# Attention values with the values standing still, two heads in the two halves of PE's columns

## The chip, the core and the metric

The kernel runs on one core of a Trainium2 chip. The metric is device time in microseconds from launch to end. Five engines work side by side and meet at semaphores: PE (matrix products; PEld is its loading of the standing operand), DVE (vector), ACT (scalar functions), POOL (here only an issuer of transfers) and SP (transfers). Each works through its own list of instructions in order.

## What is computed

One block of a decoder for 512 tokens of width 1024, in float32: a retention branch and an attention branch, both mixed by gates, and then a feed-forward layer. What matters here is the attention: 8 heads of width 64, blocks of 256 keys, of which 3 would be chosen beside a query's own block. With 512 tokens there are two blocks, so every earlier block is taken and the attention is plain causal attention:

```
mq = rmsnorm(mq, q_norm_w); mk = rmsnorm(mk, k_norm_w)        # per head, 64 wide
s_own = einsum('bhqd,bhjd->bhqj', qb, k_own) * scale           # masked where key > query
p = softmax(concatenate([s_sel, s_own], axis=-1), axis=-1)
out = einsum('bhqkj,bhqkjd->bhqd', p_sel, vs) + einsum('bhqj,bhjd->bhqd', p_own, v_own)
b = moba_attention(mq, mk, mv) @ w_moba_out
mix = sigmoid(ga) * a + sigmoid(gb) * b                        # a: the retention branch
```

## The kernel before

Nearly all of PE's work are products of activations with weights. Each operand is split into a high and a low part of type float32r, and a product is three matmuls (`mm3`). Most large products are done by a scheme of seven products in place of eight (`wino_unit`); its weights arrive as `raw` by DMA, ACT makes the high part (`wh`), DVE the low part (`wl`) and sums of weights (`wt`).

The order of everything is written out by hand. The main products go in half steps of twelve matmuls. After each half step `advance` runs what is due (`later`, then a new piece of weights), and `run_bg` takes one entry of the list `bg`, the background work. So each engine's list holds, in turn, a half step of main products, then one background entry.

The attention is such background work: 32 items (head, query tile of 128), two heads in turn, tiles 0 to 3 of a pair of heads, then the next pair. Entry `n` of the list is `att_step(n)`. With `ATT = (2, 4)` it does three things for three items:

- `att_values` for item n-4: products of `pt` with the values `mv`, 64 columns each, one per block of keys up to the diagonal; DVE writes the result, times `rl`, into `mo`
- `att_transpose` for item n-2: PE transposes the probabilities `p` block by block, ACT copies them to `pt`, DVE makes `rl = 1/l`
- `att_scores` for item n: PE makes the scores (those of two heads together for tiles 0 and 1), DVE their maximum `mx` and `nb` from it, ACT `p = exp(...)`, with the row sum `l` written when it ends

The first entry runs in the value unit `mv`, the next ones in the unit `rk` (rotary products, DVE's `rot`) and in `rv`. `mo` holds tokens by heads. Four entries `mo_steps` much later, in the last `rv` unit, transpose it (`mo_transpose`), and `split` makes the high and low part of `moT`, the input of the branch `b`. The buffers: `act` gives tiles of 512 columns out of 9, `big` tiles of 1024 columns out of 45, and PSUM has 8 banks, shared by the main products (`pm`) and the background (`ps`).

Lines of the profile: every PE and DVE instruction is recorded by a helper at L191, so tiles tell them apart. ACT's exponential is L874, the copy to `pt` L884.

Of the kernel before, what the change touches and what calls it, by code (L numbers as in the profile page):

```python
# [13 lines left out]
ALU = mybir.AluOpType  # L14
AX = mybir.AxisListType

P = 128
S = 512
D = 1024
KT = D // P  # L20
NT = S // P
# [4 lines left out]
MDH = 64  # L26
# [15 lines left out]
RLAG = (1, 2, 3)  # L42
SLAG = (1, 1, 1)
ROT = 1
MOT = 0
LATE = 1
RNORM = 4
QKS = 4
# [2 lines left out]
ATT = (2, 4)  # L51
# [87 lines left out]
def hybrid_block(ctx: ExitStack, tc: tile.TileContext, wall, xin, cin, out):  # L139
# [12 lines left out]
    def act(name, dt=F32):  # L152
        return sp.tile([P, 512], dt, name=name, tag="a")

    def big(name, dt=F32):
        return bp.tile([P, 1024], dt, name=name, tag="b")

    def halves(name, dt=F32):
        t = big(name, dt)
        return t[:, :512], t[:, 512:]  # L160

    def small(name, n, bufs=2):
        return tp.tile([P, n], F32, name=name, tag=name, bufs=bufs)
# [3 lines left out]
    def nm(s):  # L167
        uid[0] += 1
        return f"{s}_{uid[0]}"
# [4 lines left out]
    def side_ps():  # L174
        return pp.tile([P, 512], F32, name=nm("ps"), tag="bank")

    A = nc.scalar
# [22 lines left out]
    V, T = Paced(nc.vector, dve_cost), Paced(nc.tensor, pe_cost)  # L200
# [31 lines left out]
    def later(n, f):  # L232
        later_q.append([n, f])
# [122 lines left out]
    def split(name, src, scale=None, lag=0):  # L356

        lows = []

        def high():  # L360
            h, l = halves(name, F32R)
            lows.append(l)
            if scale is None:
                A.copy(h, src)
            else:
                A.activation(h, src, AF.Copy, scale=scale)
            return h

        def low(h):
            l = lows[0]  # L370
            if scale is None:
                V.tensor_tensor(l, src, h.bitcast(F32), ALU.subtract)
            else:
                V.scalar_tensor_tensor(l, src, scale, h.bitcast(F32), ALU.mult, ALU.subtract)
            return l

        p = Piece(high, low, lag, SLAG[2])
        waiting.append(p)
        return p
# [35 lines left out]
    ident = cst[:, K_ID:K_ID + P]  # L415
# [3 lines left out]
    def two(x):  # L419
        return x.rearrange("p (u c) -> p u c", u=2)  # L420
# [78 lines left out]
    for k in range(KT):  # L499
        if k % 2 == 0:  # L500
            hf[k // 2] = big(f"hf{k}")
        f = two(hf[k // 2])[:, k % 2]
        n1 = xv[:, V_N1 + k:V_N1 + k + 1]
        V.tensor_scalar(f, xt[k], n1, None, ALU.mult)
        c = slice(k % 2 * 512, k % 2 * 512 + 512)
# [58 lines left out]
    bg = []  # L564
# [252 lines left out]

    mv = {}

    mo_steps = [lambda f=f: mo_transpose(f) for f in range(4)]  # L820

    def mv_out(pair, u, x):
        for i in (0, 1):
            t = 2 * pair + i
            if i == 0 and t not in mv:
                mv[t], mv[t + 1] = halves(f"mv{t}")
            A.activation(mv[t][:, u * 256:(u + 1) * 256], x[:, i * 256:(i + 1) * 256], AF.Copy,
                         scale=st["r1"][:, t:t + 1])
        if (pair, u) == (1, 0):
            for t in (0, 2):  # L830
                mo[t], mo[t + 1] = halves(f"mo{t}")
            for n in range(len(items) + ATT[1]):
                bg.append(lambda n=n: att_step(n))
            if MOT:
                bg.extend(mo_steps)

    for _ in range(EXTRA):
        for f in load_w():
# [1 line left out]
    wino_unit(hW, Quarters(mv_out))  # L840


    mo, srg_ev = {}, {}
    items = [(2 * g + r, i) for g in range(MH // 2) for i in range(NT) for r in (0, 1)]
    att, both = {}, {}

    def score_products(h, i):

        hp, r = h // 2, h % 2
        W, d = (i + 1) * P, slice(i * P, (i + 1) * P)  # L850
        ps = side_ps()
        if i < 2:
            kh, kl = (two(x)[:, :, :W] for x in mkT[hp][:, :])
            o = ps[:, :2 * W].rearrange("p (u c) -> p u c", u=2)
            mm3(o, mqT[hp][:, d], (kh, kl), True, False)
            T.matmul(o[:, :, d], lhsT=identb, rhs=negb.unsqueeze(1).to_broadcast([P, 2, P]), start=False, stop=True)
            for x in (0, 1):
                both[2 * hp + x, i] = ps[:, x * W:(x + 1) * W]
        else:
            mm3(ps[:, :W], mqT[hp][:, d], mkT[hp][:, r * 512:r * 512 + W], True, False)  # L860
            T.matmul(ps[:, d], lhsT=identb, rhs=negb, start=False, stop=True)
            both[h, i] = ps[:, :W]

    def att_scores(h, i):
        if (h, i) not in both:
            score_products(h, i)
        W, ps = (i + 1) * P, both.pop((h, i))
        mx, nb = small("mx", 1, 4), small("nb", 1, 4)
        V.tensor_reduce(mx, ps[:, :W], AX.X, ALU.max)
        q = st["qs"][:, i * MH + h:i * MH + h + 1]  # L870
        V.tensor_scalar(nb, mx, -1.0, q, ALU.mult, ALU.mult)
        p = act(nm("p"))
        l = small("l", 1, 6)
        A.activation(p[:, :W], ps[:, :W], AF.Exp, bias=nb, scale=q, accum_out=l)  # L874
        att[h, i] = (p, l)

    def att_transpose(h, i):
        p, l = att[h, i]
        W = (i + 1) * P
        ps = side_ps()  # L880
        for j in range(i + 1):
            T.transpose(ps[:, j * P:(j + 1) * P], p[:, j * P:(j + 1) * P], ident)
        pt = act(nm("pt"))
        A.copy(pt[:, :W], ps[:, :W])  # L884
        rl = small("rl", 1, 6)
        V.reciprocal(rl, l)
        att[h, i] = (pt, rl)

    def att_values(h, i):
        pt, rl = att.pop((h, i))  # L890
        ps = side_ps()
        for j in range(i + 1):
            T.matmul(ps[:, :MDH], lhsT=pt[:, j * P:(j + 1) * P], rhs=mv[j][:, h * MDH:(h + 1) * MDH],
                     start=j == 0, stop=j == i)
        V.tensor_scalar(mo[i][:, h * MDH:(h + 1) * MDH], ps[:, :MDH], rl, None, ALU.mult)

    def att_step(n):
        if 0 <= n - ATT[1] < len(items):
            att_values(*items[n - ATT[1]])
        if 0 <= n - ATT[0] < len(items):  # L900
            att_transpose(*items[n - ATT[0]])
        if n < len(items):
            att_scores(*items[n])

    moT = {}

    def mo_transpose(f):
        ps = side_ps()
        for t in range(NT):
            T.transpose(ps[:, t * P:(t + 1) * P], mo[t][:, f * P:(f + 1) * P], ident)  # L910
        moT[f] = split(f"moT{f}", ps, None, SLAG[0])


    srg = {}
# [16 lines left out]
    def gates(n):  # L931

        ready_gates.append(n)
        for m in (0, 1):
            if ready_gates.count(m) == 2:
                ready_gates[:] = [x for x in ready_gates if x != m]
                bg.extend([None] * RGATE[m] + [lambda h=2 * m + i, p=p: ret_gate(h, p) for i in (0, 1) for p in (0, 1)])
# [52 lines left out]
    def rv_out(h0):  # L990
        def f(pair, i, x):
            rv[h0 + i, pair] = split(f"rv{h0 + i}_{pair}", x, None, 0 if (pair, i) == (1, 0) else SLAG[1])
            if (pair, i) == (1, 0):
                a, b = ([lambda h=h, j=j: ret_scores(h, j) for j in range(NT)] for h in (h0, h0 + 1))
                v, w = ([lambda h=h, p=p: ret_values(h, p) for p in range(2)] for h in (h0, h0 + 1))
                if h0 and not MOT:
                    bg.extend(mo_steps)
                bg.extend(a + b[:2] + [None, None] + v + b[2:] + [None] * 4 + w + [None])
                gates(h0 // 2)
                ret_done("rv")  # L1000
        return f
# [17 lines left out]
    def ret_scores(h, j):  # L1019

        n0 = min(j * P, 256)
        w = S - n0
        ps = side_ps()
        mm3(ps[:, :w], rkT[h][:, j * P:(j + 1) * P], rqT[h][:, n0:], True, True)
        key, off = sc_off[j]
        if off == 0:
            sc[h, key] = halves(nm("sc"), F32R)
        H, L = sc[h, key]
        d0 = j * P - n0
        s = sk[:, h * NT + j:h * NT + j + 1]  # L1030
        tmp = tp.tile([P, P], F32, name=nm("dia"), tag="dg", bufs=4)
        rest = S - (j + 1) * P
        o, d = slice(off + P, off + P + rest), slice(off, off + P)

        def first():
            V.scalar_tensor_tensor(tmp, ps[:, d0:d0 + P], s, tri, ALU.mult, ALU.mult)
            if rest:
                A.activation(H[:, o], ps[:, d0 + P:w], AF.Copy, scale=s)

        def second():  # L1040
            A.copy(H[:, d], tmp)
            if rest:
                V.scalar_tensor_tensor(L[:, o], ps[:, d0 + P:w], s, H[:, o].bitcast(F32), ALU.mult, ALU.subtract)

        later(RLAG[0], first)
        later(RLAG[1], second)
        later(RLAG[2], lambda: V.tensor_tensor(L[:, d], tmp, H[:, d].bitcast(F32), ALU.subtract))
# [343 lines left out]
```

## Time and profile before

| | |
|---|---|
| median of 3 runs | 817.28 us (816.57 to 817.59) |
| profiled execution | 817.44 us, span 815.7 us |
| PE busy | 803.1 us, 98% of the span, 5568 matmuls |
| DVE, ACT, POOL busy | 581.3, 406.3, 59.9 us |
| granted TensorE clock | 1.00 |
| attention's items, first score to last | about 88.6 to 184.8 us |
| last value products; `mo` transposed | 192.1 us; 268.8 to 274.4 us |

The span is from the first to the last instruction; the execution's own time is 1.7 us longer. A row of a group names the tile written and the tiles read (`ps<-mv,pt`), the shape, how many there are, the busy time, the mean of one in ns, and the idle time of the engine before them with what ended it. The chain is followed back from the last instruction to what released it. A single row of the timeline begins with its start and its duration in us. Matmuls are pipelined: one begins long before the one ahead has ended, so their cost in a sequence is the distance of the starts.

### The profile page before, as it was taken

To read this page: it belongs to the slowest core of one execution; us is meant where nothing else is said; L and a number is where in the kernel's file an instruction comes from. 1 tells how busy PE (TensorE), PEld (TensorE's weight loads), DVE (VectorE), ACT (ScalarE), POOL (GpSimd) and SP (SyncE) were. 2 spreads that over 40 slices of the span, in tenths; PEclk is the share of its full clock that TensorE was granted. 3 is DMA by queue.
4 is the path that set the end of the run, shared out by engine and by line. 5 is a ranking of instruction groups with operands and counts; after the bars stand their busy time and mean duration, and the time that the engine had idled before them with its cause. 6 is when DMAs were issued, how large, how long until landed. Compare 5 with 4: busy or idle time off the path is not lost.

```text
span 815.7 us, 13699 instructions
## 1 busy us (share of the span) xinstructions
PE 803.1 (98%) x5568; PEld 747.4 (92%) x5568; DVE 581.3 (71%) x889; ACT 406.3 (50%) x639; POOL 59.9 (7%) x82
## 2 busy tenths in 40 slices
PE   7998999999999999999999999999999999999998
PEld 5888999999999999998988899988999988999986
DVE  7879866786798678887666978743677665688731
ACT  8557744565447456664434466534455422455400
POOL 0004000000000000000011110000000022000000
PEclk9999999999999999999999999999999999999999
DMA  9733343162436545543747696625565676865111
GB/s 327 229 98 74 110 108 78 32 151 88 146 79 155 137 123 156 129 133 104 228 155 203 140 293 167 189 69 164 149 178 156 164 172 149 214 181 174 59 53 51
DMA packets 35839, 117.56 MB, mean 144 GB/s; under 512 B 4032, under 2 KB 4544, under 8 KB 35776
## 3 DMA queue, kind: packets, MB, share of 16 engines
q1 hardware_dynamic: 27360, 89.95, 33.4%
q0 software_dynamic: 8416, 26.74, 18.6%
q8 instruction: 43, 0.70, 0.3%
q14 instruction: 20, 0.16, 0.1%
HBM read 110.91 MB, written 4.19 MB: 141 GB/s over the span
## 4 chain that ended last, share of the span: by engine, by line
PE 95%; DVE 2%; ACT 1%; DMA 0%; issue 0%; DVEq 0%; SPq 0%; ACTq 0%
PE pm L191 86%; PE ps L191 9%; DVE wl_B L191 1%; DMA raw<-wall 0%; DVE wl_T L191 0%; ACT sqh L725 0%; ACT qk L724 0%; DVE qk L191 0%; DVE mk1l L191 0%; DVE mk0l L191 0%; DVE wt_T L191 0%; DVE ssr_y L191 0%; ACT wh_T L297 0%; DVE qb L191 0%; DVE ssr_t L191 0%
## 5 line engine op out<-in xcount | busy, mean ns | idle before, releaser
L191 PE MATMUL pm<-h2S,wh_T 128*128 128x256 f32 x528 | 96.5, 283 | 0.0
L191 PEld LDWEIGHTS pm<-h2S,wh_T 128*128 128x128 f32 x528 | 82.3, 192 | 0.0
L191 DVE TENSOR_TENSOR wl_B<-raw_B,wh_B 128x1024 fp32r<-128x1024 f32 x60 | 72.6, 1220 | 12.4 <-ACT wh_B L297 8.0
L191 DVE TENSOR_TENSOR wl_T<-wt_T,wh_T 128x1024 fp32r<-128x1024 f32 x40 | 48.9, 1223 | 43.5 <-ACT wh_T L297 41.4
L271 POOL DMA_DIRECT2D raw_T<-wall x40 | 35.0, 874 | 567.6 <-DMA raw_T<-wall 246.1
L191 PE MATMUL pm<-h2S,wl_T 128*128 128x256 f32 x264 | 74.7, 283 | 0.0
L191 PE MATMUL pm<-gh,wh 128*128 128x512 f32 x176 | 68.5, 389 | 0.0
L191 PE MATMUL pm<-gl,wh 128*128 128x512 f32 x176 | 68.5, 389 | 0.0
L191 PE MATMUL pm<-gh,wl 128*128 128x512 f32 x176 | 68.5, 389 | 0.0
L297 ACT CAST wh_B<-raw_B 128x1024 fp32r<-128x1024 f32 x60 | 62.0, 1047 | 10.8 <-PE pm L191 10.8
L191 DVE TENSOR_TENSOR wl<-raw,wh 128x1024 fp32r<-128x1024 f32 x54 | 65.5, 1219 | 1.6 <-ACT wh L297 1.3
L191 PE MATMUL pm<-h2A,wh_B 128*128 128x256 f32 x352 | 64.3, 283 | 0.0
L297 ACT CAST wh<-raw 128x1024 fp32r<-128x1024 f32 x54 | 55.4, 1044 | 11.0 <-PE pm L191 10.9
L191 DVE TENSOR_TENSOR wl_T<-raw_T,wh_T 128x1024 fp32r<-128x1024 f32 x40 | 48.8, 1221 | 16.1 <-ACT wh_T L297 10.6
L297 ACT CAST wh_T<-wt_T 128x1024 fp32r<-128x1024 f32 x40 | 41.9, 1047 | 30.9 <-DVE wt_T L191 29.4
L191 PEld LDWEIGHTS pm<-h2A,wh_B 128*128 128x128 f32 x352 | 55.1, 192 | 0.2
L297 ACT CAST wh_T<-raw_T 128x1024 fp32r<-128x1024 f32 x40 | 41.8, 1044 | 19.9 <-PE pm L191 13.2
L191 PEld LDWEIGHTS pm<-h2S,wl_T 128*128 128x128 f32 x264 | 50.7, 192 | 0.0
L191 PE MATMUL pm<-h2A,wl_B 128*128 128x256 f32 x176 | 49.8, 283 | 0.0
L191 PE MATMUL pm<-wh_T,hS 128*128 128x256 f32 x240 | 47.8, 287 | 1.2 <-ACT qa L684 1.2
L191 PE MATMUL pm<-hA,wh 128*128 128x256 f32 x256 | 47.2, 285 | 0.0
L191 PEld LDWEIGHTS pm<-wh_T,hS 128*128 128x128 f32 x240 | 39.0, 192 | 1.4 <-ACT qa L684 1.4
(276 smaller groups left out, 2153.0 us busy)
## 6 DMA issues: line engine op xcount, KB each, us to landing
raw_B<-wall SPq DMA_DIRECT2D x60, 512.0 KB, 5.1
raw<-wall SPq DMA_DIRECT2D x54, 512.0 KB, 4.1
raw_T<-wall SPq DMA_DIRECT2D x40, 512.0 KB, 3.6
raw_T<-wall POOLq DMA_DIRECT2D x40, 512.0 KB, 5.7
raw<-wall SPq DMA_DIRECT2D x8, 256.0 KB, 5.7
xr<-xin POOLq DMA_DIRECT2D x8, 256.0 KB, 5.9
x2d<-xr SPq DMA_DIRECT2D x8, 256.0 KB, 2.8
acc<-x2d POOLq DMA_DIRECT2D x8, 256.0 KB, 5.4
```

The source lines that it names most:

```text
L191: return f(out, *args, **kw)
L271: nc.gpsimd.dma_start(t[:, s], wall[c, :, s], accum_op=ALU.add)
L297: A.copy(h, src)
```

## The change

The values stand still in PE and the transposed probabilities move. For one head the standing operand is 64 columns of `mv` (one block of keys), and the moving one is `pt` for all queries from that block's own tile on: 512, 384, 256 and 128 columns. Two heads write the upper and lower 64 partitions of the same bank, which uses the two halves of PE's columns. The result of a pair of heads is `moT` as it stands, so the tile `mo` and its transposes go. For that, `pt` of a head is kept for all its query tiles (`a`, `b` in `pT[h]`), and ACT copies into it by blocks of keys. The division by the row sum moves from the result to `p`, ahead of its transposition, at the next half step (`later(1, norm)`). `att_values` runs once per pair of heads instead of once per item.

```diff
 def att_scores(h, i):
...
     A.activation(p[:, :W], ps[:, :W], AF.Exp, bias=nb, scale=q, accum_out=l)
-    att[h, i] = (p, l)
+    rl = small("rl", 1, 6)
+
+    def norm():
+        V.reciprocal(rl, l)
+        V.tensor_scalar(p[:, :W], p[:, :W], rl, None, ALU.mult)
+    later(1, norm)
+    att[h, i] = p

 def att_transpose(h, i):
-    p, l = att[h, i]
+    p = att.pop((h, i))
...
-    pt = act(nm("pt"))
-    A.copy(pt[:, :W], ps[:, :W])
-    rl = small("rl", 1, 6)
-    V.reciprocal(rl, l)
-    att[h, i] = (pt, rl)
-
-def att_values(h, i):
-    pt, rl = att.pop((h, i))
+    if i == 0:
+        pT[h] = big(nm("pt")), act(nm("pt"))
+    a, b = pT[h]
+    if i == 0:
+        A.copy(a[:, :P], ps[:, :P])
+    else:
+        A.copy(a[:, i * P:i * P + 4 * P].rearrange("p (u c) -> p u c", c=P)[:, 0:4:3, :],
+               ps[:, :2 * P].rearrange("p (u c) -> p u c", u=2))
+    if i == 2:
+        A.copy(b[:, :P], ps[:, 2 * P:W])
+    if i == 3:
+        A.copy(b[:, P:3 * P], ps[:, 2 * P:W])
+
+pT, PT = {}, ((0, 0), (0, 512), (1, 0), (1, 256))
+
+def att_values(hp):
     ps = side_ps()
-    for j in range(i + 1):
-        T.matmul(ps[:, :MDH], lhsT=pt[:, j * P:(j + 1) * P], rhs=mv[j][:, h * MDH:(h + 1) * MDH],
-                 start=j == 0, stop=j == i)
-    V.tensor_scalar(mo[i][:, h * MDH:(h + 1) * MDH], ps[:, :MDH], rl, None, ALU.mult)
+    for j in range(NT):
+        for r in (0, 1):
+            h, (x, off) = 2 * hp + r, PT[j]
+            T.matmul(ps[r * MDH:(r + 1) * MDH, j * P:], lhsT=mv[j][:, h * MDH:(h + 1) * MDH],
+                     rhs=pT[h][x][:, off:off + S - j * P], start=j == 0, stop=j == NT - 1, skip_group_check=True)
+    del pT[2 * hp], pT[2 * hp + 1]
+    moT[hp] = split(f"moT{hp}", ps, None, SLAG[0])

 def att_step(n):
     if 0 <= n - ATT[1] < len(items):
-        att_values(*items[n - ATT[1]])
+        h, i = items[n - ATT[1]]
+        if h % 2 == 1 and i == NT - 1:
+            att_values(h // 2)
...
-def mo_transpose(f):
...
-            if h0 and not MOT:
-                bg.extend(mo_steps)
```

PE's list where the first pair of heads ends. Before, at the step of item (head 1, tile 3); `pm` are main products, `mv` and `pt` the value products, `cst,p` a transposition:

```order
L191 MATMUL pm_872<-wl_T_1152,hA_195 128x256
L191 MATMUL pm_872<-wh_T_1116,hA_195 128x256
L191 MATMUL ps_1422<-mv_779,pt_1350 128x64 x2
L191 MATMUL ps_1422<-mv_915,pt_1350 128x64 x2
L191 MATMUL ps_1428<-cst,p_1358 128x128
L191 MATMUL pm_1442<-hA_113,wh_1_1231 128x256 x2
```

The same place in the changed kernel (`pt_1062` and `pt_1063` are head 0, `pt_1098` and `pt_1099` head 1):

```order
L190 MATMUL pm_872<-wl_T_1157,hA_195 128x256
L190 MATMUL pm_872<-wh_T_1124,hA_195 128x256
L190 MATMUL ps_1406<-pt_1062,mv_779 64x512
L190 MATMUL ps_1406<-pt_1098,mv_779 64x512
L190 MATMUL ps_1406<-pt_1062,mv_779 64x384
L190 MATMUL ps_1406<-pt_1098,mv_779 64x384
L190 MATMUL ps_1406<-pt_1063,mv_915 64x256
L190 MATMUL ps_1406<-pt_1099,mv_915 64x256
L190 MATMUL ps_1406<-pt_1063,mv_915 64x128
L190 MATMUL ps_1406<-pt_1099,mv_915 64x128
L190 MATMUL ps_1415<-cst,p_1343 128x128
L190 MATMUL pm_1431<-hA_113,wh_1_1230 128x256 x2
```

The pair's eight value products stand together here, and the steps of the seven items before it have none.

DVE's list at the items of tile 3 of the first two heads. Before, `rl` and the scaling of `mo` belong to items that are two and four steps older than the maximum `mx` behind them:

```order
L191 TENSOR_TENSOR wl_0_1191<-raw_0_920,wh_0_1154 128x1024
L191 TENSOR_SCALAR mo_999<-ps_1195,rl 128x64
L191 RECIPROCAL rl<-l 128x1
L191 TENSOR_REDUCE mx<-ps_1207 128x1
L191 TENSOR_SCALAR nb<-mx,qs 128x1
L191 TENSOR_SCALAR mo_999<-ps_1233,rl 128x64
L191 RECIPROCAL rl<-l 128x1
L191 TENSOR_REDUCE mx<-ps_1245 128x1
L191 TENSOR_SCALAR nb<-mx,qs 128x1
L191 TENSOR_TENSOR qb_871<-qa_870,pm_872 128x512
L191 TENSOR_TENSOR wl_1_1283<-raw_1_1003,wh_1_1231 128x1024
```

In the changed kernel:

```order
L190 TENSOR_TENSOR wl_0_1193<-raw_0_920,wh_0_1159 128x1024
L190 TENSOR_REDUCE mx<-ps_1203 128x1
L190 TENSOR_SCALAR nb<-mx,qs 128x1
L190 RECIPROCAL rl<-l 128x1
L190 TENSOR_SCALAR p_1212<-p_1212,rl 128x512
L190 TENSOR_REDUCE mx<-ps_1238 128x1
L190 TENSOR_SCALAR nb<-mx,qs 128x1
L190 TENSOR_TENSOR qb_871<-qa_870,pm_872 128x512
L190 RECIPROCAL rl<-l 128x1
L190 TENSOR_SCALAR p_1247<-p_1247,rl 128x512
L190 TENSOR_TENSOR wl_1_1279<-raw_1_1001,wh_1_1230 128x1024
```

`rl` and the scaling of `p` now stand behind the `nb` of the same item, with nothing or one subtraction (`qb`) between.

More of the change, by code (lines that the diff above doesn't have):

```diff
@@ L44 @@
 ROT = 1
-MOT = 0
 LATE = 1
@@ L818, in hybrid_block @@
     mv = {}
-    mo_steps = [lambda f=f: mo_transpose(f) for f in range(4)]
     def mv_out(pair, u, x):
@@ L829, in mv_out @@
         if (pair, u) == (1, 0):
-            for t in (0, 2):
-                mo[t], mo[t + 1] = halves(f"mo{t}")
             for n in range(len(items) + ATT[1]):
                 bg.append(lambda n=n: att_step(n))
-            if MOT:
-                bg.extend(mo_steps)
     for _ in range(EXTRA):
@@ L840, in hybrid_block @@
     wino_unit(hW, Quarters(mv_out))
-    mo, srg_ev = {}, {}
+    srg_ev = {}
     items = [(2 * g + r, i) for g in range(MH // 2) for i in range(NT) for r in (0, 1)]
@@ L905, in hybrid_block @@
     moT = {}
-    def mo_transpose(f):
[L908 to L911, printed above, removed]
     srg = {}
@@ L995, in f @@
                 v, w = ([lambda h=h, p=p: ret_values(h, p) for p in range(2)] for h in (h0, h0 + 1))
-                if h0 and not MOT:
-                    bg.extend(mo_steps)
                 bg.extend(a + b[:2] + [None, None] + v + b[2:] + [None] * 4 + w + [None])
```

## The prediction

> **What bounds the kernel now.** I read the page's first and fourth parts, then the waits of PE, then the stretch of the change.
>
> ```profile
> span 815.7 us, 13699 instructions
> PE 803.1 (98%) x5568; PEld 747.4 (92%) x5568; DVE 581.3 (71%) x889; ACT 406.3 (50%) x639; POOL 59.9 (7%) x82
> PE 95%; DVE 2%; ACT 1%; DMA 0%; issue 0%; DVEq 0%; SPq 0%; ACTq 0%
> ...
> engine line waited for: us in total, times, longest us
> PE pm L191 <- ACT mh L511: 5.7, 1, 5.7
> PE pm L191 <- ACT qa L684: 1.2, 1, 1.2
> PE ps L191 <- DVE qk L191: 0.9, 1, 0.9
> PE pm L191 <- DVE wl_T L191: 0.7, 1, 0.7
> PE ps L191 <- ACT p L874: 0.3, 1, 0.3
> ```
>
> PE is the chain, and it waits less than 10 us in all. A microsecond off PE's list is therefore a microsecond off the time, unless a new wait takes its place. The last row is the attention: one wait of 0.3 us for a `p`.
>
> The attention runs as 32 items between PE's main products. One row per stretch: the value unit (items 0 to 7), the `rk` unit (8 to 17), the rest (18 to 31). The fourth number is DVE's busy time.
>
> ```profile
> core 0: us, PE busy (x) PEld busy (x) DVE busy (x) ACT busy (x) POOL busy (x), PEclk, DMA share, GB/s
> 88.59:108.23 19.64, 19.64 (x158) 18.32 (x157) 14.80 (x35) 12.71 (x28) 0.12 (x1) 1.00 0.42 132
> 108.23:145.75 37.52, 37.52 (x314) 36.16 (x313) 25.81 (x61) 17.78 (x39) 1.60 (x2) 1.00 0.36 85
> 145.75:184.78 39.03, 38.75 (x315) 36.02 (x314) 30.36 (x76) 23.03 (x56) 1.73 (x2) 1.00 0.39 96
> ```
>
> PE is full in all three, and DVE, 71 of 96 us, has 25 us to spare. That spare time carries my argument: the change spends most of it.
>
> **The change, part by part.**
>
> *The old value products go.* Two items, one with one block of keys and one with four; the second row of each pair is where PE went on.
>
> ```profile
> 98.34 0.33 PE L191 MATMUL ps<-mv,pt 128*128 128x64 f32 x2
> 98.51 0.28 PE L191 MATMUL ps<-cst,p 128*128 128x128 f32 x1
> ...
> 115.12 1.00 PE L191 MATMUL ps<-mv,pt 128*128 128x64 f32 x8
> 115.96 0.28 PE L191 MATMUL ps<-cst,p 128*128 128x128 f32 x1
> ```
>
> Each fp32 product is two matmuls. Two cost 0.17 us, eight 0.84, so 0.11 for each further one; four and six cost 0.39 and 0.62. Eight items of each: 8 x (0.17 + 0.39 + 0.62 + 0.84) = 16.2 us, all on PE's list. With the 0.3 us wait, which sat in one of them, 16.5.
>
> *The four transposes of `mo` go.* A row of them, the next, and an ordinary half step of twelve products:
>
> ```profile
> 268.80 0.60 PE L191 MATMUL ps<-cst,mo 128*128 128x128 f32 x4
> 269.16 0.36 PE L191 MATMUL pm<-wh_T,hS 128*128 128x256 f32 x1
> 269.36 0.28 PE L191 MATMUL pm<-wl_T,hS 128*128 128x256 f32 x1
> ...
> 270.68 0.60 PE L191 MATMUL ps<-cst,mo 128*128 128x128 f32 x4
> ...
> 200.81 1.44 PE pm L191 x12
> ```
>
> The period is 1.88 us against 1.44, so 0.43 each and 1.7 for four. The split of `moT` (one ACT cast and one DVE subtraction per pair) is not saved but comes earlier, three of four within the stretch.
>
> *The new value products.* Four groups of eight, each two matmuls, with 512, 384, 256 and 128 moving columns for each of two heads: 1280 columns x 2 heads x 2 = 5120 columns a pair. No row has fp32 with more than 128 moving columns, nor half the array's columns. The nearest:
>
> ```profile
> L191 PE MATMUL ps<-mv,pt x160: 221/275/275, 95.9 to 192.8; 128*128 128x64 f32 x160
> L191 PE MATMUL ps<-dg,cst x16: 271/275/275, 55.0 to 484.4; 128*128 128x128 f32 x16
> ```
>
> The shortest with 64 columns is 221 ns, with 128 it is 275: 0.84 ns a column. One after the other, 5120 columns are 4.3 us a pair and 17.3 in all: nothing gained over 16.5. If the halves run beside each other, the order on PE (both passes of one head, then both of the other, as the list of groups has it) lets the second pass of one run with the first of the next; of each size one pass starts alone only at the beginning: (3 x 512 + 2 x 384 + 2 x 256 + 2 x 128) x 0.84 = 2.6 us a pair, 10.3 in all. Perfect pairing gives 2560 columns, 8.6. The ends are 8.6 and 17.3; no row decides, and I take 10.3, because the two heads write different partitions and need different columns. The Trainium skill's page TensorE: Matmul & The Clock Gate, Part 3, states that matmuls on distinct column groups run concurrently (three of them 2.38 times as fast); nothing in this trace shows it.
>
> *Going to halves and back*, eight times. No row has such a switch. The nearest is the end of the `mo` transposes above: the first main product behind them takes 0.20 us (269.16 to 269.36) where one in the middle takes 0.12 (1.44 for twelve). That is 0.08 a switch, 0.6 in all, and I take it. The Trainium skill's page TensorEngine Tiling (Array Packing), Key Properties, says that a change of tiling mode drains the engine. The upper end is a drain: a 256-column product lasts 0.28 us in the row above and the next starts after 0.12, so 0.16 for what is under way, 1.3 in all and 0.7 more in the sum. No run here shows it; it lies inside my own range.
>
> *DVE: `p` is scaled instead of `mo`.* Rows for the removed, and for the nearest scalings of 128 and 512 columns:
>
> ```profile
> L191 DVE TENSOR_SCALAR mo<-ps,rl 128x64 f32<-128x64 f32 x32 | 9.0, 280 | 12.1 <-PE ps L191 12.0
> L191 DVE TENSOR_SCALAR dg<-cst,r_y 128x128 f32<-128x128 f32 x8 | 1.7, 284 | 0.0
> L191 DVE TENSOR_SCALAR h2f<-xr,vec 128x512 f32<-128x512 f32 x8 | 4.0, 504 | 0.3
> ```
>
> By width 0.28, 0.35, 0.43, 0.50: 12.5 us for 32, against 9.0 removed. That is small. The place is not. `rl` now stands right behind `nb` of the same item, and it needs `l`, which ACT writes at the end of the exponential that `nb` starts. The last item, DVE and ACT in order of time:
>
> ```profile
> 183.50 0.69 DVE L191 TENSOR_REDUCE mx<-ps 128x1 f32<-128x512 f32 x1
> 184.22 0.21 DVE L191 TENSOR_SCALAR nb<-mx,qs 128x1 f32<-128x1 f32 x1
> 184.53 0.78 ACT L874 ACTIVATE p<-ps,nb,qs 128x512 f32<-128x512 f32 x1 [1.33 <-DVE nb L191]
> 185.21 0.19 ACT L874 ACTIVATION_READ_ACCUMULATOR p<-ps,nb,qs 128x1 f32 x1
> ...
> L874 ACT ACTIVATE p<-ps,nb,qs 128x384 f32<-128x384 f32 x8 | 5.4, 674 | 4.9 <-DVE nb L191 4.9
> L874 ACT ACTIVATE p<-ps,nb,qs 128x128 f32<-128x128 f32 x8 | 3.7, 467 | 2.3 <-DVE nb L191 2.2
> ```
>
> From `nb`'s start to the end of the sum is 1.18 us (185.40 - 184.22), by width 0.86, 0.97, 1.07, 1.18. DVE could go on about 0.1 after `nb`'s start, so an uncovered item stalls it 0.76, 0.87, 0.98, 1.09 us: 29.6 for 32. Everything on DVE queues behind that stall. In the changed order five items have enough other work between `nb` and `rl` (rotary products, two subtractions), hiding 4.6, and eleven have one subtraction of 512 columns, hiding 0.6 each; 18.4 us of stall stay: 5.6, 4.1 and 8.7 in the three stretches.
>
> DVE's need by stretch, from its busy time: 14.80 + 3.1 (8 scalings) - 1.1 (4 `mo`) + 5.6 = 22.4; 25.81 + 3.7 - 2.8 + 0.7 (`moT`) + 4.1 = 31.5; 30.36 + 5.7 - 3.9 + 1.4 + 8.7 = 42.3. PE's need: 19.64 - 1.1 = 18.5; 37.52 - 5.3 + 2.6 = 34.8; 39.03 - 7.2 + 2 x 2.6 = 37.0. DVE is now longer in the first and third, by 3.9 and 5.3 us. How much of it reaches PE depends on how late a `p` may be. PE transposes it two steps after its scores:
>
> ```profile
> 187.88 0.61 PE L191 MATMUL ps<-cst,p 128*128 128x128 f32 x4
> ```
>
> `p` of the last item was ready 2.5 us before (185.40). Reciprocal and scaling take 0.7 of that, and the shorter steps some 0.3, so about 1.5 us of lateness is free, once per stretch. PE then waits (3.9 - 1.5) + (5.3 - 1.5) = 6.2 us, where it waited 0.3; without any slack it would be 9.2, and nothing if the stall overlapped work I have not seen. The low halves of the weights (`wl`) stand behind the same stall. PE waited for one of them 0.7 us, once in the whole run (first rows), so they are made ahead, and I cost their delay at nothing; without that cover DVE's lag would reach PE there, in place of the wait for `p` and not on top of it.
>
> *ACT* gets sixteen more copies of about 0.27 us (the parts of `pt`), 4.3 us in a stretch where it is busy 53.5 of 96: nothing. *DMA queues*: no transfer is added or moved past another. *Later*: the retention's steps come four steps earlier; no PE wait stands there now, so nothing.
>
> *Sum*: -16.5 - 1.7 + 10.3 + 0.6 + 6.2 = -1.1. The profiled execution took 817.44 us (span 815.7 and 1.7 around it), 0.16 above the median of 817.28. So 816.2 on the scale of the median.
>
> **The rivals.**
>
> 1. *The halves don't overlap.* 17.3 instead of 10.3. PE's need in the third stretch becomes 40.4 and DVE's excess 1.9, so the waits fall to 2.4 + 0.4 = 2.8: -18.2 + 17.3 + 0.6 + 2.8 = +2.5, 819.8, slower. It decides as soon as the value groups take more than about 3.5 us each. For it: all the trace's matmuls with different weights follow each other in a pipeline, none runs beside another. Against it: only that their columns are disjoint.
> 2. *DVE's stall stays hidden.* If `p` is ready in time after all, the waits are near 0: -18.2 + 10.9 = -7.3, 810.0. For it: PE now waits 0.3 us for `p`, and DVE idles 12 us for `mo` (its row above), an idle that goes. Against it: that idle is inside the spare 25 us that I have already spent.
> 3. *The stall is dearer.* A value group of 2.6 us gives DVE no new scores, so what DVE lacks in the steps before cannot be made up in it; with no free lateness (9.2) and one microsecond more idle DVE in each of the three groups inside the stretch, the waits are 12.2: +4.9, 822.2. Half of that gives 819.2.
>
> **Chances.** My forecast 0.47, with a range of its own of 814 to 818.5 (waits 4 to 8, value groups 2.2 to 2.8 us, the drain). Rival 1: 0.25, 2: 0.15, 3: 0.13. A range of 811 to 821 leaves out half of rival 2's spread, a fifth of rival 1's and half of rival 3's, about 0.2. Within 0.2%, 1.6 us (815.6 to 818.9), a measurement of this kernel can hardly tell it from no change. Faster takes rival 2 and under half of the forecast: 0.37. Same: most of the other half and a little of the rivals, 0.29. Slower: most of rivals 1 and 3 and a tail of the forecast, 0.34.
>
> **What would show it.** The new groups `ps<-pt,mv` from first start to the next `pm`: 2.6 us each if I am right, 4.3 for rival 1. PE's waits: a row `ps` for DVE `p` of about 6 us in many pieces; near nothing for rival 2, above 9 for rival 3. DVE: idle before `rl` ended by ACT `p`, about 18 us in total. No `ps<-cst,mo` near 268 us, and `moT` ready before 200. The prediction is wrong if the rate of 0.84 ns a column doesn't hold at 512 columns, or if the free lateness of `p` is not 1.5 us: each half microsecond of it moves the result by one.

## The result, and the profile after

The changed kernel takes 825.79 us (median, 825.5 to 826.45) against 816.92 us for the kernel before on the same chip: 1.011 times as long, 95% interval 1.0092 to 1.0127. It is slower by 8.9 us. The forecast was 816.2, and its range ended at 821.

The page of the changed kernel, first and fourth part:

```profile
span 823.7 us, 13496 instructions
PE 798.6 (97%) x5456; PEld 734.1 (89%) x5456; DVE 587.0 (71%) x889; ACT 407.6 (49%) x655; POOL 59.9 (7%) x82
PE 87%; DVE 8%; ACT 2%; issue 1%; DMA 0%; SPq 0%; DVEq 0%; ACTq 0%
```

PE is busy for 4.5 us less than before (798.6 against 803.1) and the span is 8.0 us longer. PE is only 87% of the chain where it was 95%; DVE has 8% and ACT 2%. So work was saved on PE, and more was lost to waits. The waits from 85 to 230 us (in total, how often, the longest), those of PE, then of DVE and ACT:

```profile
PE ps L190 <- DVE p L190: 10.4, 11, 2.6
PE pm L190 <- DVE wl L190: 1.1, 1, 1.1
PE ps L190 <- ACT pt L893: 0.7, 1, 0.7
PE pm L190 <- ACT wh L296: 0.5, 1, 0.5
...
DVE rl L190 <- ACT p L867: 20.1, 23, 4.1
...
ACT wh L296 <- PE pm L190: 5.9, 1, 5.9
ACT wh_B L296 <- PE pm L190: 3.5, 1, 3.5
```

The first row is the wait that was forecast: PE for a scaled `p`, 10.4 us in 11 pieces. The fifth is DVE standing behind the row sums, 20.1 us. The last two were not forecast: ACT stands before casts of weights (`wh`, `wh_B`), and it is PE that it waits for, not the transfer that brings their data. A cast of weights takes nothing from PE; what it can wait for there is the tile that it will write, as long as PE still reads what is in it.

The value products, in time (one row for the eight products of a pair, 16 passes; the next row is its last two passes alone), and then their group, with the shortest, middle and longest record in ns:

```profile
117.51 0.28 PE L190 MATMUL pm<-wh_T,hA 128*128 128x256 f32 x1
117.72 2.37 PE L190 MATMUL ps<-pt,mv 128*64 128x512 f32 x16
119.82 0.28 PE L190 MATMUL ps<-pt,mv 128*64 128x128 f32 x2
120.03 0.33 PE L190 MATMUL ps<-cst,p 128*128 128x128 f32 x1
```

```profile
L190 PE MATMUL ps<-pt,mv x64: 272/432/643, 117.7 to 199.8; 128*64 128x512 f32 x16, 128*64 128x384 f32 x16, 128*64 128x256 f32 x16, 128*64 128x128 f32 x16
```

From the first start of the group to the next operation is 2.31 us (120.03 - 117.72). One after the other its 5120 columns would take 4.3 us at the 0.84 ns that the old kernel's widths gave, and paired without loss 2.15. That price holds at the larger widths: in the trace's single records the passes start in pairs, 6 to 7 ns apart, and from pair to pair it is 0.43 to 0.48 us with 512 columns and 0.32 with 384. So the two halves of the columns do run beside each other.

The longest gap of PE in the attention, with PE, ACT and DVE in order of time:

```profile
157.47 0.21 DVE L190 TENSOR_SCALAR nb<-mx,qs 128x1 f32<-128x1 f32 x1
...
159.48 0.28 PE L190 MATMUL pm<-wl_T,hS 128*128 128x256 f32 x1
159.60 0.28 PE L190 MATMUL pm<-wh_T,hS 128*128 128x256 f32 x1
159.80 1.04 ACT L296 CAST wh_B<-raw_B 128x1024 fp32r<-128x1024 f32 x1 [3.48 <-PE pm L190]
160.75 0.37 ACT L888 COPY pt<-ps 128x256 f32<-128x256 f32 x1
161.02 0.68 ACT L867 ACTIVATE p<-ps,nb,qs 128x384 f32<-128x384 f32 x1
161.58 0.20 ACT L867 ACTIVATION_READ_ACCUMULATOR p<-ps,nb,qs 128x1 f32 x1
161.82 0.16 DVE L190 RECIPROCAL rl<-l 128x1 f32<-128x1 f32 x1 [4.13 <-ACT p L867]
162.02 0.42 DVE L190 TENSOR_SCALAR p<-p,rl 128x384 f32<-128x384 f32 x1
162.49 0.55 PE L190 MATMUL ps<-cst,p 128*128 128x128 f32 x3 [2.61 <-DVE p L190]
```

Read it backwards. PE waits 2.61 us for `p`. DVE waited 4.13 us for the row sum. The exponential that makes it had its `nb` since 157.7, but ACT works in order, and ahead of it stood a cast of weights that waited 3.48 us. That cast begins at 159.80, just after the last product that reads a low half `wl_T` has ended (159.48 + 0.28 = 159.76). In the program's list of tiles the new `wh_B` is put in the very tile that held this `wl_T`. So the gap has two causes, one behind the other: a full pool of tiles holds ACT, and DVE, which now stands behind ACT, passes it on to PE. Behind the attention, DVE and PE show smaller waits:

```profile
207.58 1.23 DVE L190 TENSOR_TENSOR wl_T<-raw_T,wh_T 128x1024 fp32r<-128x1024 f32 x1 [2.81 <-PE pm L190]
...
215.81 1.21 DVE L190 TENSOR_TENSOR wl<-raw,wh 128x1024 fp32r<-128x1024 f32 x1
217.08 0.39 PE L190 MATMUL pm<-hA,wl 128*128 128x256 f32 x1 [1.13 <-DVE wl L190]
```

A low half waits 2.81 us for PE, to be written where PE still reads a `wh_B`; DVE then has no gap of its own until the `wl`, and that one is 1.13 us late for PE. That the first causes the second is not shown: with one tile more (kernel 6 below) the 2.81 us are gone and PE still waits 1.0 us for this `wl`. The longest wait of ACT, 5.9 us before the cast of `wh` at 223.97, is followed by no wait of PE and costs nothing: a long row is not yet a loss.

### The profile page after: what moved, and what is told of

It reads as the page before. It is cut to its first block, busy times and chain, and to the rows that moved or that the text cites. A ratio compares the mean times of both kernels' runs of the same rounds, so it can differ in the third digit from the quotient of the medians.

```text
span 823.7 us, 13496 instructions
## 1 busy us (share of the span) xinstructions
PE 798.6 (97%) x5456; PEld 734.1 (89%) x5456; DVE 587.0 (71%) x889; ACT 407.6 (49%) x655; POOL 59.9 (7%) x82
## 4 chain that ended last, share of the span: by engine, by line
PE 87%; DVE 8%; ACT 2%; issue 1%; DMA 0%; SPq 0%; DVEq 0%; ACTq 0%
PE pm L190 81%; PE ps L190 6%; DVE wl_T L190 1%; ACT p L867 1%; DVE wl_B L190 1%; DVE mx L190 1%; DVE p L190 1%; DVE rot L190 1%; DVE wt_T L190 1%; DVE nb L190 0%; DMA raw<-wall 0%; DVE rl L190 0%; ACT sqh L724 0%; ACT qk L723 0%; DVE qk L190 0%
## 5 line engine op out<-in xcount | busy, mean ns | idle before, releaser
L190 PEld LDWEIGHTS pm<-hA,wh 128*128 128x128 f32 x256 | 39.9, 192 | 0.7 <-ACT wh L296 0.7
```

The costliest lines, as they stand in the source:

```text
L190: return f(out, *args, **kw)
```

## Experiments

Theory 1 in the expectations is the stall: DVE stands behind each row sum. Theory 2, wherever one names it, is the pool of large tiles: the kept `pt` and the early `moT` crowd it. What else is set against them, each expectation says. Intervals are 95%, ratios are to the kernel before, on the same chip.

**1. The division one item later.** `norm` no longer runs at the next half step but behind the `nb` of the next item, when its row sum is long there; transposes and values come one entry later to leave room.

```diff
-ATT = (2, 4)
+ATT = (3, 5)
...
-        later(1, norm)
+        norms[h, i] = norm
...
 def att_step(n):
...
     if n < len(items):
         att_scores(*items[n])
+    if 0 <= n - 1 < len(items):
+        norms.pop(items[n - 1])()
...
```

> The changed kernel, with the reciprocal and the scaling of p moved behind the next item's nb on DVE, and the transposes and value products one step later. Theory 1 (DVE stands still behind each row sum, and p comes too late for PE): DVE's idle before rl falls from 20 us to under 3, PE's waits for p from 10 us to under 1, and the time is the removed 18.2 us of PE less the new 9.6: about 808 to 809.5. Theory 2 (the kept pt and the early moT crowd the 45 large buffers, so ACT's casts wait for PE and p is late behind them): the buffers are as crowded, and held a step longer, so most of the loss stays: 816 to 824.

Measured: 814.63 us, ratio 0.997 (0.9958 to 0.9983). DVE's wait for the row sum is 0.4 us where it was 20.1, and PE's for `p` 2.1:

```profile
PE ps L190 <- DVE p L190: 2.1, 2, 1.3
DVE rl L190 <- ACT p L867: 0.4, 1, 0.4
```

The same work in another place of DVE's list, with one entry more before the transposes, turns a loss of 8.9 us into a gain of 2.4. The time lies between the ranges of the two theories: the stall is gone, as theory 1 has it, but 814.6 is 5 us above what it alone allows.

**2. No division at all** (it is left out of the computation; all other work and its order stay: `dve_cost` only keeps the program's own count of DVE's load).

```diff
-        rl = small("rl", 1, 6)
...
-            V.reciprocal(rl, l)
-            V.tensor_scalar(p[:, :W], p[:, :W], rl, None, ALU.mult)
+            dve_cost(1)
+            dve_cost(W)
```

> The changed kernel with the reciprocal and the scaling of p left out, all else at its place in the order (the probabilities stay undivided). Theory 1: no stall and no scaling on DVE, PE's waits in the attention under 1.5 us, 807.5 to 809.5. Theory 2: ACT still waits for buffers ahead of the exponential, so PE waits 5 us or more for p: 813 to 820.

Measured: 817.34 us, ratio 1.0002 (0.9993 to 1.0012). This is far above what theory 1 alone allows: with no division there is no stall, and the kernel is still not faster than before. Its waits name what is left:

```profile
PE ps L190 <- ACT p L867: 3.4, 4, 2.0
PE pm L190 <- DVE wl L190: 1.1, 1, 1.1
ACT wh L296 <- PE pm L190: 7.4, 1, 7.4
ACT wh_B L296 <- PE pm L190: 2.8, 1, 2.8
```

PE waits for the exponential itself. The longest piece, 2.0 us, stands behind the same cast of `wh_B` as before, which waits 2.8 us for PE; the 7.4 us of `wh` come after the attention. The time is in theory 2's range, though PE's wait for `p` is 3.4 us and not the 5 expected there.

**3. Only the division moved, in the old kernel.** Values and `mo` stay as they were; `mo` is copied where it was scaled.

```diff
+        rl = small("rl", 1, 6)
+        def norm():
+            V.reciprocal(rl, l)
+            V.tensor_scalar(p[:, :W], p[:, :W], rl, None, ALU.mult)
+        later(1, norm)
...
-        V.tensor_scalar(mo[i][:, h * MDH:(h + 1) * MDH], ps[:, :MDH], rl, None, ALU.mult)
+        V.tensor_copy(mo[i][:, h * MDH:(h + 1) * MDH], ps[:, :MDH])
```

> The kernel before, with only the division moved: reciprocal and scaling of p at the next half step, as in the change; the values still one product per item, mo is copied by DVE without scaling, and its transposes stay. Theory 1: PE's list is unchanged, and the DVE stall of about 18 us gives new waits for p of 5 to 12 us: 822 to 830. Theory 2: the buffers are as before, and steps are long: 817 to 819.

Measured: 822.43 us, ratio 1.0066 (1.0051 to 1.0081). The division in its new place costs 5.4 us (817.08 on that chip before), with nothing else of the change. DVE has 32 operations more here than before, since `mo` is still copied; this run does not tell their part from the stall's. PE's listed waits for `p` are less than I expected:

```profile
PE ps L191 <- DVE p L191: 3.3, 7, 1.0
DVE rl L191 <- ACT p L874: 18.3, 24, 2.0
```

**4. More room for a late `p`.** The changed kernel with only `ATT = (3, 5)`: one entry more between scores and transposes.

> The changed kernel with the transposes and value products one step later and the division where the change put it (DVE's stall stays). If DVE's total need (96 us for a stretch in which PE needs 88) is the bound, one step more of lateness is paid back once per stretch, some 3 to 5 us: 820 to 823. If only the delay from scores to p is too long, and DVE has time enough, nearly all is gained: 808 to 811. Theory 2: no gain, 824 to 828.

Measured: 822.54 us, ratio 1.0062 (1.0047 to 1.0077). An entry of room gives back 3.3 of the 8.9 us; the division's place, from this kernel to the first one, gives 7.9.

```profile
PE pm L190 <- DVE wl L190: 3.4, 2, 2.4
PE ps L190 <- DVE p L190: 2.6, 3, 1.1
...
DVE rl L190 <- ACT p L867: 18.8, 24, 2.0
```

DVE has too much to do in these stretches while it stands still 18.8 us; it isn't that a `p` merely comes late once. With room for `p`, the stall reaches PE by another way: 2.4 us, at 106.64, are a wait for the low half of a weight, which stands behind the stall in DVE's list.

**5 to 7. The pool of large tiles.** These three change only how many tiles there are. Every engine's list is the same, instruction by instruction, as in the kernel that each is compared with; only which tile is reused when differs. In the old kernel, one less:

```diff
-PAIRS = 45
+PAIRS = 44
```

> The old kernel with 44 large tiles instead of 45; every engine's list stays word for word the same, only tiles are reused one tile earlier. Theory 2 (the changed kernel crowds the pool of large tiles, so that ACT and DVE wait for a tile that PE still reads, and what stands behind them is late): one tile less costs the old kernel time as well, 818.5 to 822, with new waits of ACT or DVE for PE at casts of weights. Theory 1 (only DVE's place behind the row sum matters): the old kernel has room enough, 816.5 to 817.6.

Measured: 824.82 us, ratio 1.0099 (1.0085 to 1.0112), more than either expectation. One tile less makes the old kernel nearly as slow as the change did, and by the same kind of rows as above:

```profile
PE ps L191 <- ACT p L874: 2.4, 3, 1.2
PE ps L191 <- ACT pt L884: 2.3, 2, 1.5
...
ACT wh_B L297 <- PE pm L191: 3.2, 1, 3.2
...
DVE wl_B L191 <- PE pm L191: 5.6, 2, 3.6
```

The changed kernel, one more (its place comes from two small tiles):

```diff
-PAIRS = 45
-SINGLES = 9
+PAIRS = 46
+SINGLES = 7
```

> The changed kernel with 46 large tiles instead of 45, paid for with two small ones (7 instead of 9); all lists stay the same. Theory 2: about half of what is lost beside the stall of DVE comes back, 821 to 823.5, and the cast that waits 3.5 us for PE near 160 us does so no more. Theory 1 alone: nothing changes, 825.3 to 826.3. If the two small tiles are missed, longer.

Measured: 820.41 us, ratio 1.0039 (1.0026 to 1.0051): 5.4 us of the 8.9 come back, more than I expected. The gap shown above is gone; ACT at the same place (the row of the cast has no wait):

```profile
156.99 1.03 ACT L296 CAST wh_B<-raw_B 128x1024 fp32r<-128x1024 f32 x1
157.93 0.37 ACT L888 COPY pt<-ps 128x256 f32<-128x256 f32 x1
158.56 0.68 ACT L867 ACTIVATE p<-ps,nb,qs 128x384 f32<-128x384 f32 x1 [0.26 <-DVE nb L190]
```

and its waits from 85 to 230 us:

```profile
PE ps L190 <- DVE p L190: 6.6, 9, 1.6
DVE rl L190 <- ACT p L867: 17.0, 23, 2.0
```

With the pool relieved, DVE's stall is 17.0 us and PE's wait for `p` 6.6. The same tiles without the division (left out of the computation again):

> The changed kernel without the division by the row sum (left out of the computation), with 46 large and 7 small tiles; the same lists as without the division and 45 large ones, which took 817.3. DVE no longer stands behind the row sum here, so what is left of the loss is the pool's if theory 2 holds: 810 to 814. If the loss is of another kind (the order on DVE and ACT itself, transfers), 816.5 to 818.

Measured: 811.31 us, ratio 0.9933 (0.9919 to 0.9947). One tile is worth 6.0 us here, though there is no stall that it could relieve. PE's waits are down to two rows of 1.0 us; that for `wl` behind the attention is the one that a tile doesn't remove:

```profile
PE ps L190 <- ACT p L867: 1.0, 2, 0.5
PE pm L190 <- DVE wl L190: 1.0, 1, 1.0
```

**8. Both mended.** The first kernel (division one item later) with 46 large and 7 small tiles, and with the split of a pair's result put off to where the old kernel transposed `mo`; until then four float32 half tiles are kept, in two large tiles in place of four.

```diff
-    moT[hp] = split(f"moT{hp}", ps, None, SLAG[0])
+    if hp % 2 == 0:
+        mo[hp], mo[hp + 1] = halves(f"mo{hp}")
+    A.copy(mo[hp], ps)
...
+def mo_split(f):
+    moT[f] = split(f"moT{f}", mo[f], None, SLAG[0])
+mo_steps = [lambda f=f: mo_split(f) for f in range(4)]
...
+                if h0:
+                    bg.extend(mo_steps)
```

> The changed kernel with the division one item later (which took 814.6), with 46 large and 7 small tiles, and with the result of each pair kept as one float32 half tile and split into high and low part only where the transposes of the old kernel stood, which leaves two large tiles more free from the attention to there. Theory 2: 808 to 812, as the 6.9 us won at main product 850 stay to the end instead of 2.7. Theory 1 alone: no gain over 814.6, 814 to 815.5.

Measured: 808.36 us, ratio 0.9896 (0.9882 to 0.9909). It is faster than both kernels. From 85 to 230 us no wait of PE is left in its list, and the chain is PE's again:

```profile
PE 96%; DVE 2%; ACT 1%; DMA 0%; issue 0%; SPq 0%; DVEq 0%; ACTq 0%
```

**9 to 12. What belongs to what.** The old kernel with 46 large and 7 small tiles:

> The old kernel with 46 large and 7 small tiles, its lists unchanged. It says how much of the 5.4 us that the same step gave the changed kernel belongs to the change. If the pool was already just large enough for the old kernel, 816 to 817.5; if every kernel gains alike from a tile, 812 to 814. Theory 2 in the strict form (the change crowds a pool that was large enough) expects the first.

Measured: 816.77 us, ratio 0.9995 (0.9986 to 1.0004): no difference. For the old kernel 45 tiles were just enough: one more gives nothing, one less costs 7.7 us. The first kernel with 46 and 7, without the late split:

> The changed kernel with the division one item later (814.6 with 45 large tiles) and with 46 large and 7 small tiles, without the late split. Theory 2: the tile gives back most of what is lost behind the attention, 809 to 811. If the late split alone made the 808.4 of the run before, 813 to 815.

Measured: 808.86 us, ratio 0.9901 (0.9888 to 0.9914), just below theory 2's range. The first kernel with the late split, with 45 and 9:

> The changed kernel with the division one item later and the late split, with 45 large and 9 small tiles as in the change. The late split frees two large tiles only between the attention and the split. Theory 2: the loss behind the attention (main products 900 to 1050) goes, that inside it stays, 810 to 812. If the 46th tile alone made the 808.4, 814 to 815.

Measured: 809.63 us, ratio 0.9912 (0.9899 to 0.9926), a little better than either expectation. Either relief does nearly the whole of it, by quite different means, and the second leaves the small tiles alone; both together are 0.5 and 1.3 us better than either, the first of which is within the spread of the runs. So it is the number of free large tiles that counts. The late split alone would not show that, since it also moves the casts and subtractions of `moT` out of the attention; the kernels that differ in nothing but tiles do. The third kernel (the division moved in the old one) with 46 and 7:

> The old kernel with the division moved to the probabilities (822.4 with 45 large tiles), with 46 large and 7 small tiles. If the stall of DVE costs its time by itself, 5 us above the old kernel with 46 large tiles, whatever that is: 820.5 to 823. If the stall costs time mainly through the full pool (late DVE keeps tiles longer), 1 to 3 us above it: 817.5 to 820.

Measured: 822.69 us, ratio 1.0067 (1.0054 to 1.0079), as with 45 (822.43). The moved division costs 5.9 us there with room in the pool and 5.4 without; it isn't the pool in another form.

Where the time goes: the main products come in the same order in all kernels, so the time between two of them can be compared. How much longer PE took than before from main product to main product, in us, from the starts in the traces (the stretches of the prediction are about the first three columns):

| main products | 420-528 | 528-732 | 732-900 | 900-982 | 982-1080 | 1080-1470 | 1470-1660 |
|---|---|---|---|---|---|---|---|
| before, its time | 20.7 | 37.8 | 38.3 | 14.3 | 16.9 | 51.1 | 32.0 |
| changed | +0.7 | -3.1 | +7.6 | +1.9 | +2.2 | +0.1 | -1.4 |
| changed, 46 tiles | +0.8 | -3.1 | +3.2 | +1.9 | +1.3 | 0.0 | -1.7 |
| no division | -1.8 | -3.1 | +2.1 | +1.1 | +3.7 | +0.1 | -1.4 |
| no division, 46 | -1.8 | -3.1 | -0.9 | +0.1 | +1.3 | 0.0 | -1.7 |
| only division moved | +1.6 | 0.0 | +2.1 | +1.3 | +0.1 | +0.1 | 0.0 |
| before, 44 | 0.0 | +1.2 | +5.1 | 0.0 | +0.9 | +0.1 | 0.0 |
| division later, 46, late split | -2.2 | -2.8 | -2.7 | +0.2 | -2.2 | +2.5 | -1.7 |

The pool's part (changed, 45 against 46 tiles) is 4.4 us in the third column and 0.9 in the fifth. The division's part (46 tiles, with against without) is 2.6, 0.0, 4.1 and 1.8 in the first four. The -2.2 and +2.5 in the last row belong together: with the items one entry later, 21 products of the retention move from the fifth column to the sixth.

## Why the prediction was wrong, step by step

By the medians the 8.9 us come apart like this (the old kernel is taken as 816.8, with 46 tiles; its medians on the chips used are 816.9 to 817.2). The change without division and with one tile more: 811.3 - 816.8 = -5.5. The division in its place: 820.4 - 811.3 = +9.1. The full pool: 825.8 - 820.4 = +5.4. The sum is +9.0. What the change takes from PE is more than 5.5: kernel 8, without such waits, gains 8.4. The 2.9 us between are neither the division's nor given back by the 46th tile; 2.0 of them are kernel 7's two rows of waits, and what causes these was not followed.

- **What bounds the kernel** was read rightly: PE, with almost no slack. A microsecond of listed wait was even more than a microsecond of time: from kernel 8 to the changed one the span grows 17.6 us, of which 12.8 are idle time of PE (25.1 against 12.3) and 4.8 are longer busy time (798.6 against 793.8) for the same number of products.
- **Old value products and transposes of `mo`, -16.5 and -1.7.** Right as far as the sum shows it. Without stall and crowding (kernel 8) the change gives 808.4 - 816.8 = -8.4 us. The prediction's terms with groups of 2.31 us in place of 2.6, and 0.09 for the way into each (the way out lies in the 2.31), give -16.5 - 1.7 + 9.2 + 0.4 = -8.6. The last column of the table has the transposes alone, -1.4 to -1.7.
- **New value groups, 2.6 us.** They took 2.31. The halves overlap better than I took them to, since the passes of the two heads interleave and start in pairs. Rival 1 (no overlap) fell. The rule of the Trainium skill, TensorE: Matmul & The Clock Gate, Part 3, that matmuls on distinct column groups run concurrently, agrees with this: 4.3 us of columns in 2.31.
- **Switches, 0.08 each.** Right: 0.21 us into the group (117.51 to 117.72) where a main product of 256 columns takes 0.12, whatever follows it, so 0.09; 0.21 out of it (the last pair starts at 119.82) where two passes of 128 columns take some 0.10, so 0.1. The drain that the Trainium skill states (TensorEngine Tiling (Array Packing), Key Properties) can cost no more than that here, against the 0.16 that I worked out for it.
- **DVE's stall, 18.4 us.** Right in place and size: 17.0 with room in the pool, 20.1 without.
- **How much of the stall reaches PE, 6.2 us.** Too small: 9.1. The first step that failed is the free lateness of 1.5 us in each of two stretches. In the first two stretches the forecast was 2.4 and nothing (measured 2.6 and 0.0), in the third 3.8 (4.1). But I ended the account at the last scores. Behind them PE lost another 1.8 us between main products 900 and 982, and in the old kernel with the moved division 1.3. The lateness of a `p` is not free, only due later, when the last items are transposed and no further scores give time: 1.6 us of it are one wait for a `p`, with 45 tiles (ending at 194.29 us) and with 46. My own bound without any lateness, 9.2 us, came out as the number, in part by luck: it has all of the loss in the first and third stretch.
- **The weights behind the stall and the buffers, cost at nothing.** This is the second step that failed and the larger error, 5.4 us. I looked only at PE's one wait for a `wl` (0.7 us before) and took the weights to be well ahead. What they were ahead by was the pool. `pt` of two heads now lives for eight or nine entries in up to four large tiles, and `moT` takes four large tiles where `mo` took two, from 122 us on. With 45 tiles that forces ACT and DVE to write into tiles that PE is still reading, and since ACT works in order, the exponential waits with the cast. The cover that I gave the `wl` is thin too: in kernel 4 the stall reaches PE there, with 2.4 us. The old trace has such waits already, from 85 to 230 us; I didn't read them as a sign that the pool was at its edge:

```profile
ACT wh_T L297 <- PE pm L191: 3.3, 2, 2.2
DVE wl_T L191 <- PE pm L191: 5.2, 3, 3.7
```

- **ACT's sixteen further copies, nothing.** Nearly right: in the changed kernel PE waits 0.7 us for one of them (`pt` L893); kernel 8 has the same copies and four more, and PE doesn't wait.
- **Rivals.** Rival 2 (the stall stays hidden) fell with PE's waits for `p`. Rival 3 (a dearer stall, 822.2 or 819.2) comes near the changed kernel with 46 tiles, 820.4, in number; of its two terms only the lateness that is not free is seen, not the further microsecond a group. No rival had the pool, and the range ended 4.8 us too low.
- **What would show it**: groups of 2.6 us (2.31), 18 us of DVE before `rl` (20.1), 6 us of PE for `p` (10.4, which by the prediction's own sign spoke for rival 3; 6.6 with 46 tiles), and `moT` early: the first is cast at 122.5 us, the last at 200.1, just behind the 200 forecast.

What stays open: which of the waiting casts and subtractions carry the 5.4 us was shown at one place only (the gap that ends at 162.49 us), the rest by the tiles' number alone; what the 2.9 us are that remain without the division and with 46 tiles; and a 47th tile was not tried.

## What to carry to other kernels

Count the tiles that a change holds and how long, before counting instructions: in a kernel whose pool is just large enough (45 here, where 44 costs 7.7 us and 46 gives nothing) a few tiles held longer took 5.4 of the 8.4 us that PE saved, and the bill shows up as casts that wait for PE. Put a step that needs another engine's last result behind the next item's first step, not behind its own: the same reciprocal and scaling cost 9 us in one place, and in the other, with 46 tiles, PE waits 0.5 us for them or not at all. And when a stall is given some lateness for free, follow it to the end of the stage, where it is collected.

## What the runs showed of the hardware

- Two float32 products of 64 standing columns each, in the two halves of PE's columns, run nearly at the price of one: 16 passes with 5120 columns in 2.31 us, 0.45 ns a column, where the old kernel's widths of 64 and 128 give 0.84 for one after the other (275 - 221 ns for 64 columns).
- Going from whole columns to halves and back costs about 0.1 us each way here: the first pass of a group starts 0.21 us behind a main product, where other followers start after 0.12.
- A row sum that ACT makes with its exponential is written by an instruction of its own behind it (`ACTIVATION_READ_ACCUMULATOR`, 0.20 us above, ending 0.08 us after the exponential): whoever needs the sum waits for both.
